# FFN of a macaron trunk: a third pair of chunks as seven block products, and part of the block sums on GpSimd

## The chip, the core and the metric

The kernel runs on one core of one Trainium2 chip. The metric is device time of one execution in microseconds, lower is better. The kernel before takes 937.77 us (median of three runs, 937.66 to 940.84).

## What is computed

Two layers work on x of 256 tokens by 1024, in float32. Each layer has a half-step FFN, a mixer (differential attention and mLSTM side by side) and a second half-step FFN, each between two RMSNorms:

```python
D_FF = 2816
def _swiglu(h, w_in, w_out):
    gate, up = jnp.split(h @ w_in, 2, axis=-1)
    return (jax.nn.silu(gate) * up) @ w_out

h = _swiglu(_rmsnorm(x, g[0]), ffn_w_in[l, 0], ffn_w_out[l, 0])
x = x + 0.5 * _rmsnorm(h, g[1])
```

The change concerns `h @ w_in` of the four FFNs (1024 to 2 x 2816 columns).

## The kernel before, in words

**Pieces and halves.** All weights come from HBM in pieces of 1 MB (128 x 2048 float32). TensorE computes a float32 product as three products of rounded parts: high x high, high x low and low x high. `halved` (L293) makes the two parts of half a piece (128 x 1024): ScalarE rounds it to the high part (L297), VectorE subtracts that from the raw half for the low part (L298). `fetch` (L285) issues the load of a piece on SP's queue. Raw pieces have three buffers `wr` and one `wx`, which takes every fourth piece (`raw_tile`, L383); halves have seven buffers `wl` and seven `wh`, and three of every ten halves go to a further pool (`half_tiles`, L377).

**An FFN half-step.** The 2816 hidden columns are eleven chunks of 256. A plain chunk c ("I", `in_piece`, L735) fetches two pieces, the two halves of the contraction, each with 256 gate and 256 up columns, and multiplies both with both token tiles of 128: 2 x 2 x 4 x 3 = 48 matmuls of 128 x 512. `ffn_hidden` (L655) evacuates each token tile: silu of the gate on ScalarE, and one VectorE operation of 128 x 256 (L658). The hidden tile is turned by a DMA transpose (`ffn_planes`, L661), joined on ScalarE (L674) and split into high and low (L694, L695). "O" c (`out_part`, L741) multiplies it with output piece c ("L" c): 24 matmuls into four PSUM banks `bk` that stay open over all chunks.

**A pair.** "P" c (`pair`, L784) does two chunks c and c+1 at once by a Strassen-like scheme: the blocks are token tile by half of the contraction on one side, and half of the contraction by (gate or up) on the other, and seven block products (`product`, L778, 12 matmuls each at L781) stand in for eight. The token side's sums are made once per half-step ("S" 0 to 2, `pair_tokens`, L343). The weight side's are made in `pair_blocks` (L312): blocks b11, b12, b22, b21 are four pieces; the sums b11+b12, that plus b22, b12+b22, and the running sum plus b21 are each made in two halves of 128 x 1024 by VectorE (`add`, L322, L324). The running sum lives in the tiles `qk` and `wt` (`spare`, L305), b12+b22 overwrites b12. Of the seven blocks P1 to P7 both halves are split by `halved`. The products go to two banks `pin` and two `ptr`, and five VectorE operations of 128 x 512 that read PSUM (L799, L803, L804, L810, L816), two that do not (L811, L818) and three on ScalarE make the hidden values; `pair_ready` (L822) joins and splits them after the transposes.

**Order.** `STEPS` (L37) is the written order of a half-step; chunks 4 and 5, and 8 and 9, are pairs. Chunk 10 is last: its weights are the stationary operand (`in_turned`, L747, matmuls L755 and L760), and the output chunks of `END` = 8, 9, 10 follow it. A scheduler that works when the program is built orders each engine's instructions and gives out buffers; `high_priority` lets the evacuations of a pair go ahead. In the pair itself `ready(c - 1, ...)` (L800) finishes the chunk before. The pair's own hidden values are finished at the next "I" (L905). The step "I7" of the first half-step also loads the post gain and the mixer's constants ("middle", L897 to L899); in the others "I3" does that.

GpSimd does memsets, small one-off scalings, the square roots of the norms (L539) and, in the opening, eight scalings of 128 x 256 (L476).

Of the kernel before, what the change touches and what calls it, by code (L numbers as in the profile page):

```python
# [21 lines left out]
ALU = mybir.AluOpType  # L22
# [11 lines left out]
CH = P  # L34
EPS = 1e-6
BIG = -1.0e30
STEPS = "I2 L1 S0 O0 I3 L2 S1 O1 S2 P4 L3 O2 L4 O3 I6 L5 O4 I7 L6 O5 P8 L7 O6 L8 O7 I10 L9".split()  # L37
END = (8, 9, 10)
AHEAD = 2
AT = (0, 2, 6, 6, 9, 22, 24, 24, 26, 26, 36, 40, 30, 46, 34, 50, 46, 52, 52, 57, 61, 60, 61, 67, 67, 69, 71, 78, 74, 74, 80, 84)  # L40
# [17 lines left out]
def _pack(inp):  # L58
# [9 lines left out]
    def ffn(at, l, f):  # L68
# [3 lines left out]
        order = [a[0, 0], a[0, 1], a[1, 0], a[1, 1], b[0]]  # L72
        for step in STEPS:
            c = int(step[1:])
# [10 lines left out]
    for l in range(L):  # L85
        at = l * PIECES_LAYER
        ffn(at, l, 0)
        at += PIECES_FFN
        for n, lo in enumerate(MIX_GROUPS):
            a = m_in[l][:, lo:lo + 512].reshape(2, 4, P, 512).transpose(0, 2, 1, 3)  # L90
            w[at + 2 * n:at + 2 * n + 2] = a.reshape(2, P, 2048)
        at += 2 * len(MIX_GROUPS)
        w[at:at + 4] = m_out[l].reshape(4, 2, P, D).transpose(0, 2, 1, 3).reshape(4, P, 2048)
        ffn(at + 4, l, 1)
# [43 lines left out]
class _Trunk:  # L138
# [173 lines left out]
    def pair_blocks(self):  # L312


        def fetch():
            raw = self.fetch()
            return [raw[:, j] for j in range(2)]

        def split(raw):
            return [self.halved(raw[j]) for j in range(2)]  # L320

        def add(out, a, b):  # L322
            for j in range(2):
                self.nc.vector.tensor_tensor(out[j], a[j], b[j], op=ALU.add)  # L324

        b11, b12 = fetch(), fetch()
        w = {"P1": split(b11)}
        run = self.spare()
        add(run, b11, b12)
        w["P5"] = split(run)  # L330
        b22 = fetch()
        add(run, run, b22)
        w["P6"] = split(run)
        add(b12, b12, b22)
        w["P7"] = split(b12)
        b21 = fetch()
        w["P2"] = split(b21)
        w["P3"] = split(b22)
        add(run, run, b21)
        w["P4"] = split(run)  # L340
        return w

# [388 lines left out]
    def ffn(self, pre, gi_post):  # L731
# [3 lines left out]
        def in_piece(t, kh, pin, w):  # L735
            xh, xl = xT[t][kh]
            for k in range(4):
                self.mm3(pin, xh[:, k, :], xl[:, k, :], *self.cols(w, k),
                         start=kh == 0 and k == 0, stop=kh == 1 and k == 3)

        def out_part(c, t, h, wo):  # L741
            for hf in range(2):
                for k in range(2):
                    self.mm3(po[t][hf], *h[t][k], *self.cols(wo, 2 * k + hf),
                             start=c == 0 and k == 0, stop=c == NC_FF - 1 and k == 1)
# [20 lines left out]
        def ready(c, others):  # L766
            if c in sent:
                hT = self.ffn_joined(sent.pop(c), others)
                hs[c] = self.ffn_split([hT[:, t] for t in range(NT)])

        def chunk(c, pins, behind=()):
            h = self.t2("h", (P, NT, 256))
            i = [self.ffn_hidden(pins[t], r[t], h[:, t]) for t in range(NT)]
            self.after(i[0], behind)
            send(c, h)
            ready(c - 1, i[:1])

        def product(b, x, w, new):  # L778
            for k in range(4):
                for n, (st, mv) in enumerate(((x[0], 0), (x[0], 1), (x[1], 0))):  # L780
                    self.nc.tensor.matmul(b, st[:, k, :], self.cols(w, k)[mv], start=new and k == n == 0,  # L781
                                          stop=k == 3 and n == 2, skip_group_check=True)

        def pair(c):  # L784


            tt, stt = self.nc.vector.tensor_tensor, self.nc.vector.scalar_tensor_tensor
            w = self.pair_blocks()
            b1, b2, b3, b4 = self.bank_pin(), self.bank_pin(), self.bank_tr(), self.bank_tr()
            s1, s2, s3, s4 = sums  # L790
            ahead = self.tc.high_priority
            p1, sil, u, v, h0 = self.t2("p1"), self.t2("sil"), self.t2("u"), self.t2("v"), self.t2("h")
            product(b1, xT[0][0], w["P1"], True)
            with ahead():
                i = self.nc.scalar.activation(p1, b1, AF.Copy)
            product(b4, s1, w["P5"], True)
            product(b2, s2, w["P6"], True)
            with ahead():
                tt(u, b2, p1, op=ALU.subtract)  # L799
            ready(c - 1, [i])  # L800
            product(b3, s3, w["P7"], True)
            with ahead():
                tt(v, u, b3, op=ALU.subtract)  # L803
                tt(v, v, b4, op=ALU.add)  # L804
            product(b1, xT[0][1], w["P2"], False)
            with ahead():
                self.func(sil, b1, AF.Silu, scale=r[0])
            product(b4, s4, w["P3"], False)
            with ahead():
                tt(h0, b4, u, op=ALU.add)  # L810
                stt(h0, h0, r[0], sil, op0=ALU.mult, op1=ALU.mult)  # L811
            with ahead():
                turned = [self.ffn_planes(h0)]
            product(b3, xT[1][1], w["P4"], False)
            with ahead():
                tt(u, b3, u, op=ALU.subtract)  # L816
                self.func(u, u, AF.Silu, scale=r[1])
                stt(v, v, r[1], u, op0=ALU.mult, op1=ALU.mult)  # L818
                turned.append(self.ffn_planes(v))
            sent["pair"] = c, turned  # L820

        def pair_ready(others):  # L822
            c, turned = sent.pop("pair")
            ops = [[self.ffn_operand() for _ in range(NT)] for _ in range(2)]
            for t in range(NT):
                h = self.ffn_joined(turned[t], others)
                others = [self.ffn_hilo(h[:, j], *ops[j][t])[0] for j in range(2)]
            for j in range(2):
                hs[c + j] = self.ffn_pairs(ops[j])

        hs, po, wo, sent = {}, [], {}, {}
        kept = bool(xT)
# [23 lines left out]
        else:  # L856
# [24 lines left out]
            i = self.ffn_hidden(pb1, r[1], h[:, 1])  # L881
# [3 lines left out]
        tokens = self.pair_tokens(kept, [] if kept else [self.cut_low])  # L885
        for at, step in enumerate(STEPS):
            kind, c = step[0], int(step[1:])
            if kind == "P":
                pair(c)
                swap = 1  # L890
            elif kind == "S":
                sums = next(tokens)
            elif kind == "L":
                if wo.get(c) is None:
                    wo[c] = self.piece()
            elif kind == "I":
                if c == (3 if kept else 7):  # L897
                    g = self.load_gpost(gi_post)
                    yield "middle"  # L899
                ws = [self.piece()]  # L900
                cut = self.cut
                ws.append(self.piece())
                if 0 not in wo:
                    wo[0] = self.piece()
                if "pair" in sent and c != END[-1]:  # L905
                    pair_ready([cut])
                for later in STEPS[at + 1:]:
                    if later[0] != "L":
                        break
                    wo[int(later[1:])] = self.piece()  # L910
                if c == END[-1]:
                    if "pair" in sent:
                        pair_ready([self.cut])
                    ready(c - 1, [self.cut])
                    break
                pins = [self.bank_pin() if swap else self.bank_tr() for _ in range(NT)]
                swap = 1 - swap
                for kh in range(2):
                    for t in range(NT):
                        in_piece(t, kh, pins[t], ws[kh])  # L920
                chunk(c, pins)
            else:
                if not po:
                    po = [[self.bank_bk() for _ in range(2)] for _ in range(NT)]
                for t in range(NT):
                    out_part(c, t, hs[c], wo[c])
# [572 lines left out]
```

## Time and profile before

| | |
|---|---|
| median of three runs | 937.77 us |
| the profiled execution's own time | 938.14 us |
| its span on the chip | 936.4 us |
| granted TensorE clock | 0.999 |
| busy: TensorE, VectorE, ScalarE, GpSimd | 99%, 83%, 71%, 4% |

PE is TensorE, DVE VectorE, ACT ScalarE, POOL GpSimd, SP the queue that issues the loads. A row of the profile names a line of the kernel, an engine, an operation, what it writes and reads, and how often; then busy time and the mean of one. Matmuls overlap, so the mean duration of one (0.39 us) is not the distance between two. "Idle before" is time of the engine ahead of these instructions, with what ended it. Times of windows and timelines count from the start of the span.

### The profile page before, as it was taken

How to read it: one execution, taken by the hardware profiler on the slowest of the kernel's cores; microseconds unless marked ns; L12 is line 12 of the kernel's file. 1: busy time of each engine (PE TensorE's matmuls, PEld its weight loads, DVE VectorE, ACT ScalarE, POOL GpSimd, SP SyncE). 2: the span in 40 equal slices, each digit the busy share in tenths (PEclk: the TensorE clock that was granted, in tenths of full speed). 3: DMA queues.
4: the chain of work that ended last, by engine and by line, in shares of the span. 5: the costliest groups of instructions: out<-in, count | busy, mean ns of one | idle time of the engine just before them, and what ended most of it. 6: DMA issues, size and time to landing. Idle time of an engine off the chain costs nothing.

```text
span 936.4 us, 12038 instructions
## 1 busy us (share of the span) xinstructions
PE 929.2 (99%) x4412; PEld 769.5 (82%) x4412; DVE 773.0 (83%) x1067; ACT 666.4 (71%) x1023; POOL 40.7 (4%) x66
## 2 busy tenths in 40 slices
PE   9999999999999999999999999999999999999997
PEld 6888888888888888888888888888888888888885
DVE  7999797789868899788798977968898588986974
ACT  7966876678856868676687865867778477766862
POOL 6000000000020000000000000000001000000000
PEclk9999999999999999999999999999999999999999
DMA  9947857256452956938467585474554348476531
GB/s 370 332 162 270 312 184 248 90 172 210 148 213 91 308 163 225 303 116 309 129 229 252 187 263 180 158 236 135 203 180 175 141 161 298 152 302 178 189 116 45
DMA packets 70025, 190.37 MB, mean 203 GB/s; under 512 B 45290, under 2 KB 46442, under 8 KB 49230
## 3 DMA queue, kind: packets, MB, share of 16 engines
q1 hardware_dynamic: 69246, 188.69, 59.7%
q10 hardware_dynamic: 720, 0.92, 0.3%
q8 instruction: 34, 0.56, 0.2%
q14 instruction: 25, 0.20, 0.1%
HBM read 178.06 MB, written 1.05 MB: 191 GB/s over the span
## 4 chain that ended last, share of the span: by engine, by line
PE 99%; DMA 1%; DVE 0%; ACT 0%; SPq 0%; POOLq 0%; issue 0%; DVEq 0%; ACTq 0%
PE pin L524 11%; PE pin L526 11%; PE pin L525 10%; PE bk L524 10%; PE bk L526 10%; PE bk L525 10%; PE ptr L781 9%; PE pin L781 7%; PE ptr L525 3%; PE ptr L526 3%; PE ptr L524 3%; PE ptr L755 2%; PE pin L755 2%; PE bk L502 1%; PE ptr L1123 1%; PE ptr L550 1%
## 5 line engine op out<-in xcount | busy, mean ns | idle before, releaser
L298 DVE TENSOR_TENSOR wl<-wr,wh 128x1024 fp32r<-128x1024 f32 x260 | 310.6, 1220 | 39.3 <-ACT wh L297 38.5
L297 ACT ACTIVATE wh<-wr 128x1024 fp32r<-128x1024 f32 x260 | 267.0, 1053 | 48.5 <-PE bk L526 11.6
L524 PE MATMUL pin<-wh,both 128*128 128x512 f32 x432 | 171.2, 398 | 0.0
L525 PE MATMUL pin<-wl,both 128*128 128x512 f32 x432 | 168.2, 390 | 0.0
L526 PE MATMUL pin<-wh,both 128*128 128x512 f32 x432 | 168.2, 390 | 0.0
L525 PE MATMUL bk<-wl,hh 128*128 128x512 f32 x352 | 135.9, 389 | 0.0
L524 PE MATMUL bk<-wh,hh 128*128 128x512 f32 x352 | 135.6, 390 | 0.0
L526 PE MATMUL bk<-wh,hl 128*128 128x512 f32 x352 | 133.2, 389 | 0.0
L526 PEld LDWEIGHTS pin<-wh,both 128*128 128x128 f32 x432 | 81.1, 188 | 17.3
L524 PEld LDWEIGHTS pin<-wh,both 128*128 128x128 f32 x432 | 81.3, 188 | 17.0 <-issue 0.7
L525 PEld LDWEIGHTS pin<-wl,both 128*128 128x128 f32 x432 | 81.3, 188 | 15.6
L297 ACT ACTIVATE wh<-wx 128x1024 fp32r<-128x1024 f32 x64 | 66.3, 1053 | 33.3 <-DMA wx<-in_w_dram 10.0
L298 DVE TENSOR_TENSOR wl<-wx,wh 128x1024 fp32r<-128x1024 f32 x64 | 77.2, 1219 | 13.8 <-ACT wh L297 13.8
L781 PE MATMUL ptr<-wh,both 128*128 128x512 f32 x256 | 83.8, 389 | 0.0
L526 PEld LDWEIGHTS bk<-wh,hl 128*128 128x128 f32 x352 | 66.1, 188 | 13.8
L524 PEld LDWEIGHTS bk<-wh,hh 128*128 128x128 f32 x352 | 66.1, 188 | 13.5
L525 PEld LDWEIGHTS bk<-wl,hh 128*128 128x128 f32 x352 | 66.1, 188 | 13.4
L781 PE MATMUL pin<-wh,both 128*128 128x512 f32 x192 | 63.2, 389 | 0.0
L781 PEld LDWEIGHTS ptr<-wh,both 128*128 128x128 f32 x256 | 48.0, 188 | 10.0
L525 PE MATMUL ptr<-wl,both 128*128 128x512 f32 x128 | 49.8, 389 | 0.0
L526 PE MATMUL ptr<-wh,both 128*128 128x512 f32 x128 | 49.8, 389 | 0.0
L781 PE MATMUL ptr<-wl,both 128*128 128x512 f32 x128 | 49.8, 389 | 0.0
(250 smaller groups left out, 1456.8 us busy)
## 6 DMA issues: line engine op xcount, KB each, us to landing
wr<-in_w_dram SPq DMA_DIRECT2D x130, 1024.0 KB, 5.5
wx<-in_w_dram SPq DMA_DIRECT2D x32, 1024.0 KB, 4.9
gpost<-in_gpost_dram SPq DMA_DIRECT2D x6, 512.0 KB, 6.3
wr<-in_w_dram SPq DMA_DIRECT2D x2, 512.0 KB, 5.8
x<-in_x_dram SPq DMA_DIRECT2D x2, 512.0 KB, 9.3
wr<-in_w_dram ACTq DMA_DIRECT2D x2, 256.0 KB, 4.0
wr<-in_w_dram SPq DMA_DIRECT2D x2, 256.0 KB, 5.4
wt<-in_xt_dram SPq DMA_DIRECT2D x1, 512.0 KB, 6.2
```

What stands on the lines that cost most here:

```text
L297: ia = nc.scalar.activation(hi, raw, AF.Copy)
L298: iv = nc.vector.tensor_tensor(lo, raw, hi.bitcast(F32), op=ALU.subtract)
L502: nc.tensor.matmul(pins[t], xT[t][i][lo_x][:, k], w, start=start and n == 0, stop=stop and n == 2)
L524: mm(ps, xh, wh, start=start, stop=False)
L525: mm(ps, xh, wl, start=False, stop=False)
L526: mm(ps, xl, wh, start=False, stop=stop)
L550: nc.tensor.transpose(ptr[:, k, :], x[:, (4 * hf + k) * P:(4 * hf + k + 1) * P], self.ident)
L755: self.nc.tensor.matmul(b, self.cols(w[kh], k)[0][:, c], both[kh][:, k].rearrange("p i t -> p (i t)"), start=kh == 0 and k == 0, stop=Fals ...
L781: self.nc.tensor.matmul(b, st[:, k, :], self.cols(w, k)[mv], start=new and k == n == 0, stop=k == 3 and n == 2, skip_group_check=True)
L1123: self.T(ptr[:, b, :], a[:, b * P:(b + 1) * P], self.tr.ident)
```

## The change

Chunks 6 and 7 become a pair as well; the new order has three pairs, each followed by two output chunks. `add` takes the engine, and two of the four sums (b12+b22, and the running sum plus b21) are made by GpSimd, in all three pairs. A pair's hidden values are finished in the next pair where one follows. The "middle" step of the first half-step moves to "P6".

```diff
-STEPS = "I2 L1 S0 O0 I3 L2 S1 O1 S2 P4 L3 O2 L4 O3 I6 L5 O4 I7 L6 O5 P8 L7 O6 L8 O7 I10 L9".split()
+STEPS = "I2 L1 S0 O0 I3 L2 S1 O1 S2 P4 L3 O2 L4 O3 P6 L5 O4 L6 O5 P8 L7 O6 L8 O7 I10 L9".split()
...
-        def add(out, a, b):
+        def add(engine, out, a, b):
             for j in range(2):
-                self.nc.vector.tensor_tensor(out[j], a[j], b[j], op=ALU.add)
+                engine.tensor_tensor(out[j], a[j], b[j], op=ALU.add)
+
+        dve, pool = self.nc.vector, self.nc.gpsimd
 
         b11, b12 = fetch(), fetch()
         w = {"P1": split(b11)}
         run = self.spare()
-        add(run, b11, b12)
+        add(dve, run, b11, b12)
         w["P5"] = split(run)
         b22 = fetch()
-        add(run, run, b22)
+        add(dve, run, run, b22)
         w["P6"] = split(run)
-        add(b12, b12, b22)
+        add(pool, b12, b12, b22)
         w["P7"] = split(b12)
         b21 = fetch()
         w["P2"] = split(b21)
         w["P3"] = split(b22)
-        add(run, run, b21)
+        add(pool, run, run, b21)
         w["P4"] = split(run)
...
             ready(c - 1, [i])
+            if "pair" in sent:
+                pair_ready([i])
             product(b3, s3, w["P7"], True)
...
             if kind == "P":
+                if c == 6 and not kept:
+                    g = self.load_gpost(gi_post)
+                    yield "middle"
                 pair(c)
...
-                if c == (3 if kept else 7):
+                if c == 3 and kept:
```

## Rows read from the trace of the kernel before

**Rows 1.** The page: span, busy time, granted clock by slice, chain that ended last.
```profile
span 936.4 us, 12038 instructions
...
PE 929.2 (99%) x4412; PEld 769.5 (82%) x4412; DVE 773.0 (83%) x1067; ACT 666.4 (71%) x1023; POOL 40.7 (4%) x66
...
PEclk9999999999999999999999999999999999999999
...
PE 99%; DMA 1%; DVE 0%; ACT 0%; SPq 0%; POOLq 0%; issue 0%; DVEq 0%; ACTq 0%
```
**Rows 2.** Waits of TensorE, whole span: us in total, times, longest.
```profile
PE bk L513 <- PEq L1489: 0.8, 1, 0.8
```
**Rows 3.** The chain in order of time: start, us, what.
```profile
365.24 5.44 PE ptr L781 x24
```
**Rows 4.** Windows from chunk 4's pair to the last in-projection: busy us by engine.
```profile
48.00:153.00 105.00, 105.00 (x465) 86.92 (x464) 93.94 (x105) 75.68 (x93) 1.69 (x3) 1.00 0.67 239
328.10:439.40 111.30, 111.30 (x492) 92.19 (x491) 97.06 (x106) 78.57 (x94) 0.00 (x0) 1.00 0.67 220
502.70:615.80 113.10, 113.10 (x501) 93.65 (x499) 96.13 (x106) 81.22 (x98) 0.00 (x0) 1.00 0.64 211
789.80:902.20 112.40, 112.40 (x497) 93.08 (x496) 96.73 (x105) 80.70 (x98) 0.00 (x0) 1.00 0.61 204
```
**Rows 5.** Waits: two of the second window, then VectorE's on landings, whole span.
```profile
DVE wl L298 <- ACT wh L297: 12.6, 10, 3.5
ACT wh L297 <- PE ptr L781: 7.1, 5, 3.3
...
DVE wr L324 <- DMA wr<-in_w_dram: 10.4, 4, 3.7
```
**Rows 6.** VectorE's timeline: five splits one behind the other.
```profile
82.69 5.76 DVE L298 TENSOR_TENSOR wl<-wr,wh 128x1024 fp32r<-128x1024 f32 x5
```
**Rows 7.** Groups by line and shape: count, busy us, mean ns, idle before.
```profile
L298 DVE TENSOR_TENSOR wl<-wr,wh 128x1024 fp32r<-128x1024 f32 x260 | 310.6, 1220 | 39.3 <-ACT wh L297 38.5
L297 ACT ACTIVATE wh<-wr 128x1024 fp32r<-128x1024 f32 x260 | 267.0, 1053 | 48.5 <-PE bk L526 11.6
...
L658 DVE SCALAR_TENSOR_TENSOR h<-pin,rs,sil 128x256 f32<-128x256 f32 x30 | 14.2, 478 | 3.2 <-ACT sil L269 3.2
...
L818 DVE SCALAR_TENSOR_TENSOR v<-v,rs,u 128x512 f32<-128x512 f32 x8 | 6.0, 744 | 0.0
...
L803 DVE TENSOR_TENSOR v<-u,ptr 128x512 f32<-128x512 f32 x8 | 5.4, 678 | 0.0
```
**Rows 8.** Line L469 on VectorE, in the opening: min/median/max ns.
```profile
L469 DVE SCALAR_TENSOR_TENSOR both<-wt,aT,both x4: 697/698/703, 10.2 to 13.9; 128x256 fp32r<-128x256 f32 x4
L469 DVE SCALAR_TENSOR_TENSOR both<-qk,aT,both x3: 470/472/484, 6.4 to 9.0; 128x256 fp32r<-128x256 f32 x3
```
**Rows 9.** Timelines of GpSimd and VectorE in the opening: start, us.
```profile
8.57 2.53 POOL L476 TENSOR_SCALAR qk<-qk,c_gpre 128x256 f32<-128x256 f32 x2 [0.57 <-DVE both L469]
11.08 2.48 POOL L476 TENSOR_SCALAR wt<-wt,c_gpre 128x256 f32<-128x256 f32 x2
...
9.00 0.47 DVE L469 SCALAR_TENSOR_TENSOR both<-qk,aT,both 128x256 fp32r<-128x256 f32 x1
...
12.31 4.74 POOL L476 TENSOR_SCALAR wt<-wt,c_gpre 128x256 f32<-128x256 f32 x3
...
15.13 2.54 DVE L298 TENSOR_TENSOR wl<-wr,wh 128x1024 fp32r<-128x1024 f32 x2
```
**Rows 10.** VectorE's timeline after the second window: the splits left.
```profile
440.32 2.35 DVE L298 TENSOR_TENSOR wl<-wr,wh 128x1024 fp32r<-128x1024 f32 x2
```
**Rows 11.** VectorE's timeline, second half-step: pair 4's last hidden tile.
```profile
394.33 0.42 DVE L695 TENSOR_TENSOR hl<-hT,hh 128x256 fp32r<-128x256 f32 x1
```
**Rows 12.** Third half-step, second pair: sum b12+b22, and the last product.
```profile
574.74 2.36 DVE L324 TENSOR_TENSOR wr<-wr,wr 128x1024 f32<-128x1024 f32 x2 [3.66 <-DMA wr<-in_w_dram]
...
608.48 2.72 PE ptr L781 x12
```

## The prediction

> **What bounds the kernel now.** I read the page's sums first. TensorE is busy for 929.2 of 936.4 us at full clock, the chain that ended last is 99% TensorE [rows 1], and the only wait of the TensorE queue in the whole trace is 0.8 us at the start [rows 2]. So no wait is there to be removed: the time falls only if TensorE gets less to do, and rises as soon as another engine is late for it. Inside the chain 24 block-product matmuls take 5.44 us, 0.2267 us each with no gap [rows 3]; that is the price of one matmul.
>
> Then I asked who could become late. The windows view, cut for each of the four FFN half-steps from VectorE's first work on chunk 4's pair to the start of the last chunk's in-projection (the first L755 of the half-step), gives VectorE 93.9 to 97.1 us of work in 105.0 to 113.1 us [rows 4]: it is idle for 11.1, 14.2, 17.0 and 15.7 us, 57.9 in all. ScalarE has some 30 us spare in each. VectorE is the engine to watch: it makes the low half of every weight block, the sums of blocks, and the evacuations. In the second window 12.6 us of its idle time end with ScalarE's high half, and ScalarE there waits for TensorE to release a buffer [rows 5]: the splits run ahead as far as the buffers allow. That is the cover which the change spends.
>
> **TensorE: less work, certain.** Chunks 6 and 7 as plain chunks take 2 chunks x 2 halves of the contraction x 2 token tiles x 12 = 96 matmuls; as a pair they take 7 products x 12 = 84. Four half-steps save 48 x 0.2267 = 10.9 us, 2.72 us in each window. The pieces fetched stay four of 1 MB, so the traffic is the same. Against the profiled execution's own 938.14 us (0.4 us over the median of the runs, so the same to within what matters) the time without any new wait is 927.2 us.
>
> **VectorE: what is added and taken away in each window.** One split costs 1.135 us when they follow each other: five take 5.76 us, the last of them 1.22 [rows 6, 7]. A pair splits 14 half-blocks where two plain chunks split 8: +6 x 1.135 = +6.8 us. Sums: before, two pairs had 8 half-sums each on VectorE, 16; now three pairs have 4 each, 12: -4.5 us. Evacuation: a pair has five at 0.68 and two at 0.74 us, 4.9 us, where two plain chunks had four at 0.48, 1.9 us [rows 7]: +3.0. Net +5.3 us. With the window 2.7 us shorter, VectorE's idle time falls by 8.0 us in each: to 3.1, 6.2, 9.0 and 7.7 us, 25.9 in all. ScalarE gets six more casts of 1.05 us and three larger evacuations, which its spare time hides.
>
> **GpSimd: twelve new half-sums in each window.** No row shows a sum of two 128x1024 blocks on GpSimd. What one does to VectorE has a near row. In the opening, GpSimd scales 128x256 tiles (L476) beside VectorE's L469, which has two inputs in SBUF. L469 takes 0.47 us undisturbed and 0.70 us in the four cases beside GpSimd [rows 8], and two splits in a row, usually 2.35 us [rows 10], take 2.54 beside the last of them [rows 9]. So VectorE loses 0.19 to 0.23 us for 256 elements of one GpSimd input. The sum reads two inputs of 1024 elements: 8 x 0.23 = 1.84 us lost per half-sum, more than the 1.135 us that VectorE would need to make it itself. Lower end: only one input counts, 0.92 us; lower still, nothing, if VectorE's turn came first each time. Upper end: GpSimd's instruction runs 1.24 us [rows 9], and if all of that scaled with length alone, 5.0 us. I take 1.84, since L469 measures the loss itself. Operations that read PSUM (15 evacuations of 0.68 us, 10.2 us, a tenth of VectorE's time) I let run free: 12 x 1.84 x 0.9 = 19.9 us per window, 79.5 in all.
>
> The Trainium skill (SBUF — State Buffer, Who interferes with whom) says that a VectorE instruction with two SBUF inputs and a GpSimd instruction that reads SBUF exclude each other for the whole instruction. The rows agree that one waits for the other, but L469 lost 0.23 us to an instruction of 1.24 us, so they do not show a block for all of it. The skill's GPSIMD Engine Reference (Elementwise, side-by-side cycle accounting) has 4497 ns for an add of 2048 float32; halved, an estimate of 2.25 us per half-sum, which as a full block would put this sum at about 982 us.
>
> **The sum.** 79.5 us lost less 25.9 us idle leaves VectorE 53.6 us late. It may spend its lead: when the last in-projection starts in the second window only two splits are still to come [rows 10], so of the ten half-blocks of chunk 10 and of the output pieces 8, 9 and 10 eight are ready, while two are needed at once; six splits may slip, 6.8 us per window, 27.2 in all. That leaves 26.4 us. But 10.4 us of the old idle time is VectorE waiting for the pair's third block to land [rows 5], and I keep that: 36.8 us of TensorE waits. 938.1 - 10.9 + 36.8 = **964 us**. If none of the lead can be spent it is 991.
>
> **What is moved.** The finishing of pair 4's hidden values moves from chunk 6 into pair 6's products, and output chunks 4 and 5 follow the pair. Pair 4's last product ends at 370.7 us and its last hidden tile is split by 394.8 [rows 3, 11], 24 us; after the change the rest of output chunk 3 and the pair's 84 matmuls (19.0 us) lie between, about 25 us, and the first half of output chunk 4 uses the other token tile: nothing, with little to spare. The constants of the first half-step and its post gain move ahead of pair 6's four fetches on SP's queue, behind nothing that is due; at worst the longest wait for a landing, 3.7 us [rows 5], once, which the lead covers. On GpSimd's queue the sums stand behind small one-off work and ahead of the square roots of the norms, which come a whole chunk later.
>
> **Rivals.**
> (1) Not slower: GpSimd's reads slip into VectorE's gaps and take nothing. For it: VectorE has 25.9 us left over, and the L469 at 9.00 us kept its 0.47 us while a GpSimd instruction was under way [rows 9]. Against it: the four at 0.70 us in a row, where VectorE had no gaps, which is how it stands here. It decides below (25.9 + 27.2) / 43 = 1.2 us lost per half-sum (48 half-sums x 0.9 = 43). Time 927 us.
> (2) One input's worth, 0.92 us: 39.7 us lost, inside idle time and lead; the waits for landings (10.4 us) become visible instead. 938.1 - 10.9 + 10.4 = 938 us, no change that can be told.
> (3) The sums come late rather than taking VectorE's time. The four half-sums of a pair run one behind the other on GpSimd. Between the sum of the second and fourth block and the last product lie 33.7 us [rows 12], so each may take 8.4 us. L476 scaled by eight is 9.9 us; at 9 us each pair is 2.3 us late, 12 pairs 27 us: 954 us. Against it: most of L476's 1.24 us is waiting for VectorE and start-up, which do not scale.
> (4) The change works as written but other queues stumble (the order is made by a scheduler ahead of time, and a cast waiting for a late sum holds up ScalarE's queue): slower, some 945 to 960 us.
>
> **How the numbers follow.** A measurement can tell about 0.5%, 4.7 us. The forecast, VectorE held by GpSimd's reads, has 0.55; (1) 0.28; (2) 0.08; (3) 0.05; (4) 0.04. Faster: 0.28 and a quarter of (2), 0.30; same: the rest of (2) and a little, 0.07; slower 0.63. The forecast's own range is 945 to 990 us; with (1) the range reaches down to 926.
>
> **What would show it.** Right: TensorE busy falls by 10.9 us while the span grows; new waits of TensorE on VectorE's low halves inside the three pairs; splits of L298 stretched from 1.22 us to 2.5 us and more while a GpSimd sum runs; VectorE without idle time in the windows. Wrong: split durations still at 1.22 us beside GpSimd's sums, and no TensorE wait (rival 1); ScalarE's casts of summed blocks waiting for GpSimd while splits keep 1.22 us (rival 3). If the time is under 930 us, the step that failed is the 1.84 us per half-sum.

## The result: 1019 us, slower by 8.5%

The changed kernel takes 1019.12 us (median of 4 runs, 1016.28 to 1019.53) against 937.87 (937.66 to 940.84): ratio 1.0852, 95% interval [1.0823, 1.0881]. The direction was forecast, the size was not: 81 us more instead of 26, and above the upper end of the range.

The page of the kernel after, for [rows 1]:
```profile
span 1014.3 us, 12163 instructions
...
PE 942.8 (93%) x4364; PEld 767.9 (76%) x4364; DVE 869.5 (86%) x1087; ACT 688.1 (68%) x1043; POOL 227.0 (22%) x114
...
PEclk9999898999999999998999997999999999998999
...
PE 6%; DVE 4%; issue 1%; POOL 1%; ACT 0%; POOLq 0%; DVEq 0%; ACTq 0%
```
TensorE has the 48 matmuls less (4364 against 4412), and yet its busy time is up by 13.6 us, to 942.8. The span grew by 77.9 us, and this line splits it: TensorE is not busy for 1014.3 - 942.8 = 71.5 us where it was for 7.2 before, **64.3 us more**; the other 13.6 are **24.5 us more** for the same matmuls, less the 10.9 us saved. The clock line says where the 24.5 come from: it has fallen below 9 in five slices, where it was 9 throughout. The last line, the chain that ended last, adds up to 12% only: it could not be followed further back, so it doesn't say what bounds the whole run.

The same four windows after the change, from pair 4's first sum to the last in-projection, for [rows 4]: the stretch, its length, busy us of TensorE, its weight loads, VectorE, ScalarE and GpSimd, then the granted clock.
```profile
48.30:174.90 126.60, 108.37 (x448) 86.11 (x448) 121.30 (x112) 82.56 (x99) 49.21 (x15) 0.95 0.58 195
349.80:478.90 129.10, 114.38 (x482) 91.71 (x481) 121.63 (x113) 87.00 (x102) 47.71 (x12) 0.96 0.57 186
544.00:674.80 130.80, 113.92 (x481) 91.16 (x480) 121.28 (x113) 85.58 (x101) 47.94 (x14) 0.96 0.56 185
849.70:980.10 130.40, 115.97 (x482) 93.10 (x481) 121.60 (x113) 86.81 (x102) 43.31 (x12) 0.95 0.55 176
```
Nearly all of the loss is here. The four lengths add up to 516.9 us (441.8 before), VectorE's work to 485.8 (383.9 before), 102.0 more, where the prediction's terms said 21.2 + 79.5 = 100.7. So the work that VectorE got was forecast almost exactly (over the whole span it is 869.5 - 773.0 = 96.5 more). But VectorE is still idle for 516.9 - 485.8 = 31.1 us of the same windows in which TensorE waits for it.

Waits of TensorE, whole span, in place of the single one of [rows 2]: us in total, times, longest.
```profile
PE ptr L783 <- DVE v L807: 29.5, 7, 9.8
PE pin L783 <- DVE wl L298: 17.5, 13, 5.2
PE ptr L783 <- DVE wl L298: 6.4, 7, 1.4
PE pin L783 <- ACT wh L297: 4.1, 2, 3.2
PE bk L526 <- ACT hh L696: 3.7, 2, 2.0
```
L783 is the block product (L781 before). The largest wait is not one for a weight split: L807 is the evacuation v = u - b3 that must have read its PSUM bank before the pair's last product adds to it. It costs VectorE 0.67 us, but it stands in VectorE's queue behind splits, and those stand behind GpSimd.

VectorE's splits and GpSimd's sums, two views by group: count, busy us, mean ns, idle time before. First the split's own line on the page of the kernel after, for [rows 7]:
```profile
L298 DVE TENSOR_TENSOR wl<-wr,wh 128x1024 fp32r<-128x1024 f32 x260 | 338.8, 1328 | 31.3 <-ACT wh L297 31.0
```
Then GpSimd's largest groups, by form, and min/median/max ns of two of them:
```profile
L324 POOL TENSOR_TENSOR qk<-qk,wr 128x1024 f32<-128x1024 f32 x12 | 63.0, 5250 | 58.8 <-DVE wl L298 55.3 <-issue 3.6
L324 POOL TENSOR_TENSOR wr<-wr,wr 128x1024 f32<-128x1024 f32 x16 | 60.7, 3814 | 200.1 <-DMA wr<-in_w_dram 102.0 <-ACT wh L297 51.6 <-DVE qk L324 31.2
L324 POOL TENSOR_TENSOR wt<-wt,wr 128x1024 f32<-128x1024 f32 x12 | 36.0, 3001 | 20.3 <-DVE wl L298 20.3
...
L324 POOL TENSOR_TENSOR qk<-qk,wr x12: 2399/3655/11914, 62.4 to 945.8; 128x1024 f32<-128x1024 f32 x12
L324 POOL TENSOR_TENSOR wt<-wt,wr x12: 2339/3276/3400, 66.4 to 954.2; 128x1024 f32<-128x1024 f32 x12
```
One half-sum lasts 3.0 to 5.3 us on GpSimd in the mean, because each engine holds the other up. One stretch of the second half-step shows both sides. GpSimd's timeline (start, us):
```profile
445.05 8.52 POOL L324 TENSOR_TENSOR qk<-qk,wr 128x1024 f32<-128x1024 f32 x1 [5.83 <-DVE wl L298]
453.53 3.33 POOL L324 TENSOR_TENSOR wt<-wt,wr 128x1024 f32<-128x1024 f32 x1
```
VectorE's timeline of the same stretch:
```profile
446.69 4.62 DVE L298 TENSOR_TENSOR wl<-wr,wh 128x1024 fp32r<-128x1024 f32 x4
451.24 0.68 DVE L801 TENSOR_TENSOR u<-pin,p 128x512 f32<-128x512 f32 x1
451.84 2.82 DVE L298 TENSOR_TENSOR wl<-wr,wh 128x1024 fp32r<-128x1024 f32 x1
454.70 3.24 DVE L298 TENSOR_TENSOR wl<-qk,wh 128x1024 fp32r<-128x1024 f32 x1
...
460.13 0.67 DVE L807 TENSOR_TENSOR v<-u,ptr 128x512 f32<-128x512 f32 x1
```
The first half-sum of GpSimd (8.52 us) lasts past VectorE's four splits, which keep their usual pace; then a split takes 2.82 us instead of 1.22, and beside the second half-sum one takes 3.24. L807 comes after all of it.

The times show how the two hold each other up. The split of 451.84 ends at 454.66, 1.1 us after the first half-sum (453.57); the one of 454.70 ends at 457.94, 1.1 us after the second (456.86): each waited until GpSimd was through and then took nearly its usual time. In the whole trace 43 of the 48 half-sums stretch one VectorE instruction each, by 1.80 us in the mean and 2.22 at most, and 39 of these 43, the splits and sums of 128x1024, end 1.08 to 1.09 us after the half-sum. The other four are of 128x256, from L697, end 0.28 us after it, and lose up to 2.2 us like the large ones, so the loss goes by GpSimd's instruction and not by VectorE's:
```profile
L697 DVE TENSOR_TENSOR hl<-hT,hh x80: 407/416/2634, 35.5 to 985.8; 128x256 fp32r<-128x256 f32 x80
```
L801, which reads one input from PSUM, keeps its 0.68 us in the middle of this, and the half-sum of 8.52 us ends 2.33 us after L801 begins, just the length of the shortest: it got its turn there.

Last, the clock. Windows of the kernel after, columns as above, around waits of the fourth half-step:
```profile
913.00:923.70 10.70, 6.27 (x22) 3.66 (x20) 10.70 (x10) 10.70 (x13) 1.61 (x1) 0.92 0.74 259
923.70:929.00 5.30, 5.24 (x13) 4.14 (x14) 5.30 (x8) 2.43 (x5) 0.00 (x0) 0.53 0.74 267
929.00:936.30 7.30, 7.30 (x34) 6.03 (x33) 4.77 (x7) 2.13 (x2) 6.07 (x2) 1.00 0.64 212
```
And the chain of waits of the kernel after (start, us, what):
```profile
923.76 5.31 PE ptr L783 x12
...
933.62 2.72 PE ptr L783 x12
```
TensorE had stood still for 4.4 of the 10.7 us; the next twelve matmuls had all they needed and took 0.44 us each, at a granted clock of 0.53, the 1.2 GHz level; ten microseconds later twelve take 0.227 each again. The clock is lower in every window, 0.95 or 0.96 (the four lines of windows above) against 1.00 before [rows 4]; as the matmuls are the same otherwise, I put the 24.5 us down to it.

### The profile page after: what moved, and what is told of

The parts are those of the page before. It is cut to its first block, busy times and chain, and to the rows that moved or that the text cites. A ratio compares the mean times of both kernels' runs of the same rounds, so it can differ in the third digit from the quotient of the medians.

```text
span 1014.3 us, 12163 instructions
## 1 busy us (share of the span) xinstructions
PE 942.8 (93%) x4364; PEld 767.9 (76%) x4364; DVE 869.5 (86%) x1087; ACT 688.1 (68%) x1043; POOL 227.0 (22%) x114
## 5 line engine op out<-in xcount | busy, mean ns | idle before, releaser
L298 DVE TENSOR_TENSOR wl<-wr,wh 128x1024 fp32r<-128x1024 f32 x260 | 338.8, 1328 | 31.3 <-ACT wh L297 31.0
L783 PE MATMUL ptr<-wh,both 128*128 128x512 f32 x384 | 135.5, 416 | 31.7 <-DVE v L807 29.5
L526 PE MATMUL pin<-wh,both 128*128 128x512 f32 x368 | 146.5, 400 | 0.0
L528 PE MATMUL pin<-wh,both 128*128 128x512 f32 x368 | 143.8, 391 | 0.0
L527 PE MATMUL pin<-wl,both 128*128 128x512 f32 x368 | 143.4, 390 | 0.0
L783 PEld LDWEIGHTS ptr<-wh,both 128*128 128x128 f32 x384 | 77.6, 202 | 52.3 <-DVE v L807 32.8
L324 POOL TENSOR_TENSOR wr<-wr,wr 128x1024 f32<-128x1024 f32 x16 | 60.7, 3814 | 200.1 <-DMA wr<-in_w_dram 102.0
L297 ACT ACTIVATE wh<-qk 128x1024 fp32r<-128x1024 f32 x36 | 38.2, 1062 | 93.9 <-DVE qk L324 48.2
L783 PE MATMUL pin<-wh,both 128*128 128x512 f32 x288 | 96.9, 396 | 4.1 <-ACT wh L297 4.1
L298 DVE TENSOR_TENSOR wl<-wx,wh 128x1024 fp32r<-128x1024 f32 x64 | 81.3, 1284 | 6.6 <-ACT wh L297 6.6
L783 PE MATMUL ptr<-wl,both 128*128 128x512 f32 x192 | 80.1, 417 | 6.4 <-DVE wl L298 6.4
L528 PEld LDWEIGHTS pin<-wh,both 128*128 128x128 f32 x368 | 69.1, 188 | 14.8
L526 PEld LDWEIGHTS pin<-wh,both 128*128 128x128 f32 x368 | 69.3, 188 | 14.5 <-issue 0.7
L527 PEld LDWEIGHTS pin<-wl,both 128*128 128x128 f32 x368 | 69.2, 188 | 13.1
```

The source lines that it names most:

```text
L297: ia = nc.scalar.activation(hi, raw, AF.Copy)
L298: iv = nc.vector.tensor_tensor(lo, raw, hi.bitcast(F32), op=ALU.subtract)
L324: engine.tensor_tensor(out[j], a[j], b[j], op=ALU.add)
L526: mm(ps, xh, wh, start=start, stop=False)
L527: mm(ps, xh, wl, start=False, stop=False)
L528: mm(ps, xl, wh, start=False, stop=stop)
```

## The experiments

Three theories were set against each other: (A) GpSimd's reads stop VectorE; (B) the third pair is the cost, whoever makes the sums; (C) the sums on GpSimd come late. The kernel before was timed beside each group of runs, at 938.0 to 939.2 us.

**1. Three pairs, all sums on VectorE.**
```diff
-        dve, pool = self.nc.vector, self.nc.gpsimd
+        dve = pool = self.nc.vector
```


> Three pairs, all four sums of each on VectorE, nothing on GpSimd. Theory A (GpSimd's reads hold VectorE up): without them VectorE has 54.5 us more sums of its own (48 x 1.135) but loses none of the 78.6 us that it lost beside GpSimd's sums, so it is some 29 us short over four half-steps, about what its lead can take: 927 to 945 us, TensorE waits under 20 us in all, splits at 1.22 us, TensorE's clock granted in full. Theory B (three pairs in a row are too much for VectorE whoever makes the sums): over 1000 us, with the same waits of TensorE on low halves and evacuations.

Measured: 990.08 us, ratio 1.0547 [1.0526, 1.0568]; splits at 1.22 us again. The page of this kernel:
```profile
PE 942.6 (95%) x4364; PEld 768.1 (78%) x4364; DVE 845.1 (85%) x1135; ACT 687.9 (70%) x1043; POOL 41.0 (4%) x66
```
Its two longest waits of TensorE (us in total, times, longest):
```profile
PE bk L526 <- ACT hh L696: 22.1, 7, 5.3
PE pin L783 <- DVE wl L298: 6.1, 8, 1.2
```
A miss for A alone and for B alone: 990 lies above A's range and below B's. Without any sum on GpSimd, three pairs still cost 63 us over the 927 that TensorE's work would allow, but the largest wait is now for the hidden values of the chunks (hh, L696) before the output chunk that needs them, and not for low halves, as B had it. The change as made is 29 us slower still, and that part is GpSimd's.

**2. The kernel before, with two of its pairs' four sums on GpSimd.**
```diff
...
-        add(b12, b12, b22)
+        add(b12, b12, b22, self.nc.gpsimd)
...
-        add(run, run, b21)
+        add(run, run, b21, self.nc.gpsimd)
```


> The kernel before (two pairs, chunks 6 and 7 plain), with the same two sums of each pair on GpSimd: 32 half-sums. Theory A: VectorE loses 32 x 1.64 = 52 us to GpSimd and is rid of 36 us of sums, 16 us more in windows that have 58 us idle: 938 to 955 us, splits beside GpSimd stretched to over 3 us as in the change. Theory B: no change, 938 us, since there is no third pair. Theory C (the sums come late and hold up ScalarE's casts): ScalarE's casts of the summed blocks wait for GpSimd, and 945 to 965 us.

Measured: 956.85 us, ratio 1.0199 [1.0177, 1.0220]. The page of this kernel:
```profile
PE 934.8 (98%) x4412; PEld 770.8 (81%) x4412; DVE 800.7 (84%) x1035; ACT 663.7 (69%) x1023; POOL 135.9 (14%) x98
```
VectorE has 32 half-sums less to make, 36.3 us at 1.135, and is busy for 27.7 us *more* than before (773.0). It lost 64.0 us to 32 half-sums, 2.0 each. So B alone falls as well: the sums on GpSimd cost time even where the pairs are as they were. A's range is missed by 2 us, and 956.85 lies in C's; but C's sign is not there: ScalarE's casts wait 1.9 us for a sum of GpSimd in this trace, and 36.1 us for sums of VectorE (10.3 before).

**3 and 4. The change with one of the two sums back on VectorE.**
```diff
-        add(pool, run, run, b21)
+        add(dve, run, run, b21)
```


> Three pairs, GpSimd makes b12+b22 alone (24 half-sums), VectorE the running sum plus b21. Theory A: 24 x 1.64 = 39 us lost to GpSimd and 27 us of sums back on VectorE, 40 us short in all before the lead: 955 to 990 us, the same as with the other sum on GpSimd. Theory C: close to all-VectorE, since this sum has more than 10 us before its products.

```diff
-        add(pool, b12, b12, b22)
+        add(dve, b12, b12, b22)
```


> Three pairs, GpSimd makes the running sum plus b21 alone (24 half-sums), VectorE b12+b22. Theory A: as many half-sums as with b12+b22 alone, so the same time within 10 us, 955 to 990 us. Theory C (late sums): this is the sum that stands last before the last product and waits for the splits of the block before, so it is clearly slower than the other one, by 20 us or more.

Measured, one execution each: 983.5 us with b12+b22 alone on GpSimd, 1001.8 with run+b21 alone. They are 18 us apart, where A had at most 10 and C 20 or more, so neither is borne out, and neither sum is the whole of it. The first is 7 us under run 1 though its VectorE is busier (851.2 against 845.1 us): TensorE's waits there are many and short (the largest group 18.8 us in 16, and no wait over 2.5), and its granted clock is 0.984 against 0.974. With single executions I read no more from it than that where a delay falls is worth some microseconds either way.

**5. The change with GpSimd's two sums left out.**
```diff
-        add(pool, b12, b12, b22)
...
-        add(pool, run, run, b21)
```


> The change with the two sums of GpSimd left out and made by no one (P7 and P4 then use unsummed blocks, so the hidden values are other numbers; TensorE, ScalarE and the splits do the same work as in the change). Theory A (it is VectorE's time that is short): VectorE has 30.6 us of work for 29.9 us of TensorE in each pair with its two output chunks, so hardly a wait: 927 to 942 us, clock in full. Theory B (three pairs in a row leave nothing to fill the time until a pair's hidden tiles are ready, whoever makes the sums): TensorE still waits for hidden tiles and evacuations, over 960 us.

Measured: 937.05 us, ratio 0.9982 [0.9972, 0.9991]. The page of this kernel:
```profile
PE 921.3 (99%) x4364; PEld 759.0 (81%) x4364; DVE 793.0 (85%) x1087; ACT 685.5 (73%) x1043; POOL 39.2 (4%) x66
```
This run and the two around it give the two prices with the same instructions on VectorE otherwise. After the change VectorE is busy for 869.5 - 793.0 = 76.5 us more, lost beside 48 half-sums, **1.59 us each**; in run 1 it is 845.1 - 793.0 = 52.1 us more, 48 half-sums made by VectorE itself, **1.09 us each**.

**6. Run 5, and GpSimd reads the same blocks into a tile that nobody waits for.** GpSimd adds the blocks in pieces of 256 columns; two fill sizes are cut to make room for the tile, here and in runs 7, 10 and 11.
```diff
...
+                for k in range(0, 1024, 256):
+                    pool.tensor_tensor(self.dummy, a[j][:, k:k + 256], b[j][:, k:k + 256], op=ALU.add)
...
+        idle_sum(b12, b22)
...
+        idle_sum(run, b21)
```


> As with the sums left out, but GpSimd does add the same blocks, each half-sum as four sums of 256 columns into a tile of its own that nobody reads: the same reads by GpSimd, and no engine waits for a result. Theory A: the reads alone hold VectorE up, by some 1.6 us per half-sum, 78 us in all: splits stretched, 985 to 1020 us, near the change. Theory C (the change is slow because ScalarE's casts and VectorE wait for late sums): within 10 us of the run with the sums left out.

**7. Run 5, and GpSimd only writes that tile**: eight columns copied, then eight memsets of 128x256 for each half-sum.
```diff
...
+                pool.tensor_copy(self.dummy[:, 0:8], b[j][:, 0:8])
+                for k in range(8):
+                    pool.memset(self.dummy, 0.0)
```


> As before, but in place of each half-sum GpSimd reads eight columns and then writes a tile of its own eight times (128x256 each), some 2.5 us of GpSimd without reads. Theory A (it is GpSimd's reads that hold VectorE): splits stay at 1.22 us and the time is within 5 us of the run with the sums left out. If any work of GpSimd holds VectorE up: splits stretched and 985 us or more.

Measured: run 6 takes 1024.09 us, ratio 1.0916 [1.0868, 1.0964]; run 7 takes 937.19 (one execution). The splits of one tile, min/median/max ns, in run 6:
```profile
L298 DVE TENSOR_TENSOR wl<-wt,wh x36: 1207/1741/1766, 55.3 to 968.6; 128x1024 fp32r<-128x1024 f32 x36
```
The same splits in run 7:
```profile
L298 DVE TENSOR_TENSOR wl<-wt,wh x36: 1206/1218/1232, 54.7 to 883.0; 128x1024 fp32r<-128x1024 f32 x36
```
And the page of run 7, where GpSimd (POOL) is busy for 213.7 us:
```profile
PE 921.2 (98%) x4364; PEld 758.9 (81%) x4364; DVE 793.2 (85%) x1087; ACT 686.1 (73%) x1043; POOL 213.7 (23%) x498
```
So late results are not needed for the loss: nobody waits for GpSimd's results in run 6, VectorE is busy for 77.7 us more than in run 5 (76.5 in the change), 0.40 us for each of the 192 pieces, and the time is that of the change. And it is the reads: a GpSimd about as busy with writes as the change's is moves neither a split nor the time. C is not down to nothing by that. In run 6 the next loads still wait for GpSimd to be through with the blocks:
```profile
SPq L290 <- POOL dummy L333: 38.4, 8, 9.1
```
In the change itself ScalarE's casts wait 18.7 us in all for GpSimd's sums, and the short chain that can be followed back goes through one of them for 8.5 us. What share of the time that is was not measured; TensorE's two largest waits, in the change and in run 6 (28.1 and 21.8 us), are for VectorE. The Trainium skill (SBUF — State Buffer, Who interferes with whom) says that a VectorE instruction with two SBUF inputs contends with a GpSimd instruction that reads SBUF, and not with one that only writes there; both halves agree with these two runs.

**8. Three pairs that do not follow each other**, sums on VectorE: the pairs stand at chunks 2, 5 and 8, each with a plain chunk after it.
```diff
-STEPS = "I2 L1 S0 O0 I3 L2 S1 O1 S2 P4 L3 O2 L4 O3 P6 L5 O4 L6 O5 P8 L7 O6 L8 O7 I10 L9".split()
+STEPS = "L1 S0 O0 S1 S2 P2 L2 O1 I4 L3 O2 P5 L4 O3 L5 O4 I7 L6 O5 P8 L7 O6 L8 O7 I10 L9".split()
...
-        dve, pool = self.nc.vector, self.nc.gpsimd
+        dve = pool = self.nc.vector
...
```


> Three pairs with all sums on VectorE, but not in a row: chunks 2 and 3, 5 and 6, 8 and 9 are pairs, 4, 7 and 10 plain between them. The work is that of three pairs in a row with the sums on VectorE (990 us). If VectorE's total is what is short there, the same 980 to 1000 us; if it is that the pairs stand in a row, with VectorE over its share for three cycles and no plain chunk in which to catch up, then the saving of 10.9 us shows: 927 to 945 us.

Measured: 988.30 us, ratio 1.0531 [1.0505, 1.0558], run 1's time within the scatter of both. That the pairs stand in a row is not the cause. VectorE's work for three of them is what is left, and runs 5 and 9 bear it out, though leaving out a sum also takes away the wait of a cast for it.

**9. The change with all four sums left out.**
```diff
-        add(dve, run, b11, b12)
...
-        add(dve, run, run, b22)
...
-        add(pool, b12, b12, b22)
...
-        add(pool, run, run, b21)
```


> The change with all four sums of each pair left out (P4 to P7 then use unsummed blocks, so the hidden values are other numbers; everything else as in the change). Against the run with two sums left out (937 us) VectorE is rid of another 24 sums, 54 us in all. If the 10 us that stood there between 937 and the 927 of the sum are VectorE's too: 926 to 930 us and no TensorE waits. If they are the wait for a pair's hidden tiles, with no plain chunk between two pairs: 935 to 938 us as before.

Measured: 927.19 us, ratio 0.9880 [0.9864, 0.9897]. The page of this kernel:
```profile
PE 918.0 (99%) x4364; PEld 760.7 (82%) x4364; DVE 742.5 (80%) x1039; ACT 690.8 (75%) x1043; POOL 40.0 (4%) x66
```
All of TensorE's waits in it:
```profile
PE bk L511 <- PEq L1492: 0.8, 1, 0.8
```
The gain of the 48 matmuls is real, 11.3 us by the medians where 10.9 were forecast, as soon as VectorE is early enough. The 10 us that run 5 lacks of it go with VectorE's other two sums.

**10 and 11. The kernel before, with 43 us more work for VectorE**: 128 adds of 128x256 into an unused tile, in run 10 at the pairs' sums, in run 11 at plain chunks.
```diff
...
+        idle_sum(b12, b22)
...
+        idle_sum(run, b21)
```


> The kernel before with 32 half-sums more on VectorE, in the two pairs (each as four sums of 256 columns into a tile of its own that nobody reads; 0.335 us each in a row, 1.34 us per half-sum, 43 us in all). If VectorE's idle time in the windows (58 us) and its lead can be spent, as the forecast had it: 938 to 943 us. If they cannot, since the idle time comes after the pairs and not before them (the run with two pairs and GpSimd's sums: 30 us more for VectorE, 19 us more in time): 960 to 985 us.

```diff
...
+                for hi, lo in ws[1]:
+                    for k in range(0, 1024, 256):
+                        self.nc.vector.tensor_tensor(self.dummy, hi.bitcast(F32)[:, k:k + 256], lo.bitcast(F32)[:, k:k + 256], op=ALU.add)
```


> The kernel before with the same 43 us of extra VectorE work, but at the plain chunks 2, 3, 6 and 7 (two half-sums' worth each, of the halves just made). If the idle time lies between the pairs and can be spent there: 938 to 945 us, clearly faster than with the work in the pairs. If VectorE has no time to give anywhere in the half-step: the same as with the work in the pairs, 960 us or more.

Measured: 949.95 us, ratio 1.0137 [1.0097, 1.0177], and 944.64, ratio 1.0065 [1.0048, 1.0082]. By their pages VectorE is busy for 42.2 and 40.6 us more. So even in the kernel before, with 57.9 us of idle time in the windows [rows 4], the same work costs 11.5 us at one place and 6.2 at another. Run 10 lies between the two ranges that were set for it, run 11 just inside the lower one: part of the idle time can be spent, and not all. Run 10 also costs less time than run 2 (11.5 against 18.8 us by the medians) though VectorE got more to do (42.2 against 27.7 us). So the total of VectorE's work does not set the time alone; whether it is the stretches of up to 2.2 us in single splits that make the difference was not tested.

**12. Three of the sums made by adding DMAs from GpSimd's queue**, the one candidate that would relieve VectorE of sums without GpSimd's reads.
```diff
...
+        def land(out, n):
+            for j in range(2):
+                pool.dma_start(out[j], self.a["w"][at[n]][:, j * 1024:(j + 1) * 1024], accum_op=ALU.add)
...
-        add(dve, run, run, b22)
+        land(run, 2)
...
-        add(pool, b12, b12, b22)
+        land(b12, 2)
...
-        add(pool, run, run, b21)
+        land(run, 3)
```


> Three pairs, b11+b12 on VectorE, the other three sums of each pair made by DMA: transfers issued from GpSimd's queue that add the block, read once more from HBM, onto the tile (6 of 512 KB per pair, 3 MB more traffic per pair; 203 GB/s before, some 240 after). VectorE is rid of 12 half-sums per half-step against the change's 12 that it kept 12 of: between the run with two sums left out (937 us) and the one with all left out (927 us), some 930 us, if the adding transfers land in time (their blocks have 10 us and more) and their making does not hold VectorE up. If they land late, or are slow because they read and write the tile: over 950 us, with ScalarE's casts waiting for DMA.

Measured: 1040.62 us, ratio 1.1069 [1.1039, 1.1099]. Waits of ScalarE and of TensorE in this kernel (us in total, times, longest):
```profile
ACT wh L297 <- DMA qk<-in_w_dram: 76.8, 15, 8.8
...
PE pin L790 <- ACT wh L297: 41.3, 9, 9.8
```
Its DMA issues from GpSimd's queue (KB each, median us to landing):
```profile
wr<-in_w_dram POOLq DMA_DIRECT2D x24, 512.0 KB, 10.2
qk<-in_w_dram POOLq DMA_DIRECT2D x24, 512.0 KB, 7.7
```
VectorE is busy for 767.3 us only and the splits keep 1.22, but a sum now lands 8 to 10 us after its issue, and the casts wait for it. None of the versions tried beats the kernel before, but for those that leave sums out.

**All runs side by side**, from their pages. VectorE: its busy time over that of before, plus 10.9 us where there are three pairs, as TensorE's time is shorter by that. TensorE idle: span less busy, over the 7.2 us of before. Clock: TensorE's busy time over 929.2 (918.3 with three pairs).
```
run                         VectorE  TensorE idle  clock   (us)
9  no sums                    -19.6       -0.1     -0.3
2  two pairs, GpSimd sums      27.7       13.4      5.6
5  two sums left out           30.9        6.6      3.0
11 before, more at plain       40.6        4.4      2.1
10 before, more at pairs       42.2        7.0      3.5
1  three pairs, VectorE        83.0       38.8     24.3
8  three pairs apart           85.3       43.2     21.4
3  b12+b22 on GpSimd           89.1       35.9     20.3
4  run+b21 on GpSimd           98.3       47.2     27.3
   the change                 107.4       64.3     24.5
6  reads, nobody waits        108.6       61.6     36.7
```
What is left of the first column after the other two was taken up without delay: 9 us in run 2, 10 to 34 in the others, 18.6 in the change (if the clock is left out of it, as in the forecast, 14, 24 to 53 and 43). It is no fixed amount, and in the six runs that had more than 74.7 us to take up it was never near the 74.7 (57.9 idle + 27.2 lead - 10.4 kept) on which the forecast counted. (Run 7 is as run 5; run 12 is held up by landings.)

## Why the prediction was wrong in size

**TensorE's gain: right.** 10.9 us, 927.2 without new waits; run 9 measures 927.19.

**VectorE's net work and its loss to GpSimd: right in size.** 5.3 us of net work in each window and 79.5 us of loss in all were forecast, 100.7 together; the windows show 102.0, the whole span 96.5: 20.0 of net work (run 5 against before) and 76.5 of loss (the change against run 5). The price of 1.84 us for a half-sum, with nine tenths exposed 1.65, measured 1.59; by place it was 1.3 (run 3) to 2.0 (run 2). That the evacuations run free also holds: L801 and L807 keep 0.67 to 0.68 us. The way there was not shown, though. The forecast scaled the loss of a small instruction in the opening [rows 8] by eight, and found a block for the whole GpSimd instruction not shown by its rows; the trace of the change shows VectorE waiting to the end of the half-sum, 43 times of 48 and 1.80 us in the mean. That the two numbers agree is in part luck: L469 lost 0.23 us to a GpSimd instruction of 1.24, a stretched split 1.80 to one of 2.34 and more. The forecast's reason, that the price exceeds the 1.135 us that VectorE needs itself, is the core of that part of the result: run 2 shows it without a third pair. The Trainium skill's GPSIMD Engine Reference (Elementwise, side-by-side cycle accounting) gave an estimate of 2.25 us for a half-sum by itself; the shortest of the 48 here took 2.34, so that agrees. The mean loss, 1.59, is less than that although VectorE waits to the half-sum's end: five of the 48 stretched nothing, and a split that comes up in the middle of one waits only for the rest.

**The idle time and the lead: the step that failed.** "79.5 us lost less 25.9 us idle", and "It may spend its lead", 27.2 us. The windows show what became of both. Of 57.9 us of idle time 31.1 are still idle, so 26.8 were spent where the forecast, keeping only the 10.4 us of landings, spent 47.5. And of the lead nothing was spent. VectorE's timeline after the second window of the changed kernel, whose last in-projection starts at 478.90, for [rows 10]:
```profile
477.61 1.23 DVE L298 TENSOR_TENSOR wl<-wx,wh 128x1024 fp32r<-128x1024 f32 x1 [0.55 <-ACT wh L297]
479.51 1.22 DVE L298 TENSOR_TENSOR wl<-wr,wh 128x1024 fp32r<-128x1024 f32 x1 [0.67 <-ACT wh L297]
481.67 1.22 DVE L298 TENSOR_TENSOR wl<-wr,wh 128x1024 fp32r<-128x1024 f32 x1 [0.94 <-ACT wh L297]
```
Two splits (479.51 and 481.67) are still to start at that point, as before the change; the other three windows show two as well, before and after. VectorE arrives there just as early; the delay had been paid in TensorE's waits inside the pairs. I had measured the lead at the window's end, where nobody needs it, and not at the products in the pairs, where a split, or the evacuation L807 queued behind it, is due. So the windows grew by 102.0 less 26.8, 75.1 us, where the forecast's terms give 100.7 - 47.5 - 27.2 = 26.0. (That the first sum comes out is bookkeeping, a window being work and idle time, and proves nothing by itself.) These 49 us, 27.2 of lead, 20.7 of idle time and 1.3 of work, are all but 3 of the 52 between the forecast of 964 and the profiled 1016.28; without the lead the forecast itself had 991.

Why the 31.1 us stay idle is seen in part: 5.2, 5.3, 9.3 and 6.1 us of it end with ScalarE's high half, and ScalarE itself waited, for sums and for buffers that TensorE held. VectorE's instructions run in the order in which the scheduler wrote them, and these gaps were not filled. That this also sets how much is spendable was not tested by itself.

**The clock: a form of the loss that was not foreseen.** The sum turned VectorE's lateness into TensorE's waits one for one. It had 36.8 us of waits; 64.3 came, and the matmuls after them ran for some time at the 1.2 GHz level, 24.5 us more: 64.3 + 24.5 - 10.9 gives the 77.9 us by which the span grew. The kernel before, with no waits, has 9 in every slice of the clock line [rows 1], so this could not be seen in it. It is not the change's own: run 1, with other waits, pays 24.3. But it is not a further item on top of VectorE's account, which gives 75.1 of the 77.9 us without it: both are the same growth, seen from two engines. Behind the wait that ends at 923.76 the chain runs on through TensorE, so the 2.6 us that the twelve matmuls lost lie on it; elsewhere TensorE at full clock might only have come to the next wait sooner. No run shows which part of the 24.5 us a full clock would have given back.

**The moved step: wrong too, though it didn't decide here.** "Nothing, with little to spare" was said of the hidden values that now finish inside pair 6. In run 1 TensorE waits 22.1 us for hidden values; in the change it is 3.7; that the waits in the pairs come first there and give that work its time fits, but was not tested.

**The rivals.** (1), reads that take nothing: refuted by the stretched splits and by run 6. (2), one input's worth: the loss is 1.59, not 0.92. (3), late sums: not needed, as run 6 shows, where nobody waits for them, and TensorE's largest waits name VectorE; a share by way of ScalarE, whose casts wait 18.7 us for them, stays open. (4), stumbling queues: the 29.5 us behind L807 are of that kind, but come from VectorE's lateness, as run 5 without GpSimd's reads has 2.4 us of it. The forecast's signs came true but two: VectorE is not without idle time, and TensorE's busy time, which should have fallen by 10.9 us, rose with the clock.

## What to carry to other kernels

Moving an elementwise add with two inputs in SBUF from a busy VectorE to GpSimd made VectorE busier here: each 128x1024 half-sum took 1.3 to 2.0 us from it, by run, and spared it 1.1, since VectorE's next instruction with two such inputs waited until GpSimd was through. Idle time in a window is not a budget: run 10 took up 32 of 42 us without delay, the change 18.6 of 107. Measure how early an engine's results are at the very instruction that consumes them, in the place where the load is added, and count as spendable only that. And where TensorE has never waited, waits alone understate what lateness does to it: 64 us of waits came with 24.5 us at the lower clock. Add the two when you count on TensorE's side, and neither when you have counted VectorE's lateness already.

## What the runs showed that was not expected

- GpSimd can be made to wait out several VectorE instructions: its half-sum of 8.52 us lasted past four splits, and the longest took 11.91, against 2.34 us for the shortest of the 48. So the hold-up goes both ways, and a single split then loses up to 2.2 us.
- GpSimd's writes cost VectorE nothing that shows: 174 us more of GpSimd's work in run 7 left the splits at 1.22 us.
- The adding DMA from GpSimd's queue took 7.7 to 10.2 us for 512 KB (run 12), where the plain fetches from SP's queue in the same kernel took 6.2 and 7.0 us for 1 MB.
